# Multi-query attention on one core: the order of the queues comes from a virtual-time planner, and GpSimd's part of each cube is placed beside VectorE's passes over PSUM

## The chip, the core and the metric

The kernel runs on one core of a Trainium2 chip. A core has five engines that each work through a queue of their own: TensorE (PE in the profile; its weight loads are listed apart as PEld), VectorE (DVE), ScalarE (ACT), GpSimd (POOL) and SyncE (SP, which here only issues DMAs). They wait for each other through semaphores. SBUF is the on-chip memory that all engines and the DMAs use, PSUM the small accumulator memory that TensorE writes and VectorE and ScalarE read. The metric is the device time of one execution in microseconds; less is better. It is a little longer than the profile's span, which runs from the first to the last instruction of the program.

## The reference

Eight batches, 1024 positions, 16 query heads of 64, and one shared key and value head per batch:

```python
    q = q.transpose(0, 2, 1, 3)
    k = k[:, None, :, :].copy()
    v = v[:, None, :, :].copy()
    scores = np.matmul(q, k.transpose(0, 1, 3, 2)) / np.sqrt(head_dim)
    weights = np.exp(scores - np.max(scores, axis=-1, keepdims=True))
    weights = weights / np.sum(weights, axis=-1, keepdims=True)
    attn_out = np.matmul(weights, v)
    return attn_out.transpose(0, 2, 1, 3).astype(np.float32)
```

q is (8, 1024, 16, 64), k and v are (8, 1024, 64), all float32; the output has q's shape.

## The kernel before

**Steps.** The work is cut into 1024 steps u. A step is one pair of heads p (64 over all batches), one of two chunks c of 512 queries and one of eight tiles j of 128 keys. Eight steps of one pair and chunk make what is called a half here. In a step TensorE computes the scores of both heads (L261): two matmuls with 64 rows each into one PSUM tile `sc` of 128 keys x 2 heads x 512 queries. Such a tile takes two PSUM banks and there are three of them, so at most three steps' scores exist at a time. The scores leave TensorE transposed, keys on partitions, ready to be the weights of the second matmul. No maximum is subtracted; the sums of the weights are checked instead, and a slow general path stands ready behind a flag.

**Two ways to take the exponential.** ScalarE does it in one activation (L274) from `sc` to an fp16 tile `wt` (24 buffers). In every fifth step, 200 in all, VectorE does it with integer operations, which is called a unit here:

- bits (L215): scores plus an offset, from PSUM, written as int16; read as fp16 this is a rough power of two
- mantissa (L221) and power (L231): the mantissa and the exponent bits of that, by bit masks, from SBUF to SBUF
- square (L242): the mantissa times itself
- the cube: bits times square, 1024 columns of which GpSimd makes columns 512 to 1023 (L243) and VectorE columns 0 to 511 (L249, called rest below)

Bits, power and cube are three weight tiles in `w3` (6 buffers), and the values are kept three times, scaled by 1, C0 and C3 (L206, prep_v), so that three value matmuls add up to the exponential's. A step on ScalarE has one term, a unit three.

**Values.** A half has eight groups (4 blocks of 128 queries x 2 heads). Each sums its terms over the half's eight steps in matmuls of 128x65 (L335; the 65th column is the sum of the weights). Seven groups share a PSUM bank; two banks alternate. When seven are complete VectorE takes the reciprocals of the sums (L277, inverse) and multiplies (L286, finish) into `osb`, and SyncE stores what is complete, a half at a time. The last half is done apart (L365).

**Order.** Each engine's queue is in the order in which the program records its instructions. Before, this order is a fixed pattern: `step(u)` records the scores and the activation or the bits pass, then up to two pending VectorE operations; after three steps of every five (`DEAL`) a number of value matmuls worked out by `plan()` follows, some 18 scores behind (`LAG`). GpSimd's half of the cube is recorded with the square and starts whenever that is done.

**Next batch.** While a batch runs, the next one is loaded: keys and, on GpSimd's queue, values (L108) and eight q tiles (L125); SyncE transposes q by DMA (L135), and `prep_k` scales k on GpSimd into a doubled fp16 copy (L194, two instructions) which SyncE transposes (L198).

Of the kernel before, what the change touches and what calls it, by code (L numbers as in the profile page):

```python
# [24 lines left out]
DEAL = (1, 1, 0, 1, 0)  # L25
DEAL_AT = 1
VE_U = 512
VE_N = 1
VE_M = 5
# [3 lines left out]
def attention_main(ctx, tc, q, k, v, out, flag):  # L33
# [23 lines left out]
    OCH = 7  # L57
# [8 lines left out]
    wtp = ctx.enter_context(tc.tile_pool(name="wtp", bufs=24))  # L66
    w3p = ctx.enter_context(tc.tile_pool(name="w3p", bufs=6))
    mp = ctx.enter_context(tc.tile_pool(name="mp", bufs=2))
    osbp = ctx.enter_context(tc.tile_pool(name="osbp", bufs=2))
    chkp = ctx.enter_context(tc.tile_pool(name="chkp", bufs=2))  # L70
    scp = ctx.enter_context(tc.tile_pool(name="scp", bufs=3, space=PSUM))
# [9 lines left out]

    kv = {}
# [4 lines left out]
    ot = {}  # L87
    pend = []
    product = []
    late = []  # L90
    checked = [0]
# [98 lines left out]
    def prep_k(b):  # L190
        st = kv[b]
        k16d = kvp.tile([P, NKT, 2, D], FP16, tag="k16d", name=f"k16d_{b}")
        for i in range(2):
            nc.gpsimd.tensor_scalar(  # L194
                out=k16d[:, :, i, :], in0=st["knat"], scalar1=kscale, scalar2=None, op0=ALU.mult
            )
        st["k2t"] = kvp.tile([P, S], FP16, tag="k2t", name=f"k2t{b}")
        nc.sync.dma_start_transpose(  # L198
            out=st["k2t"].rearrange("p (j s) -> p j s", j=NKT),
            in_=k16d.rearrange("p j i d -> p (j i d)"),  # L200
        )

    def prep_v(b):
        vp = kv[b]["vp"]
        for i, ci in ((1, C0), (2, C3)):
            nc.vector.tensor_scalar(  # L206
                out=vp[:, i, :, 0:D], in0=vp[:, 0, :, 0:D], scalar1=ci, scalar2=None, op0=ALU.mult
            )

    def vector_exp(sc, p, c, j):  # L210
        w3 = w3p.tile([P, 3, 2, QCH], FP16, tag="w3", name=f"we{p}_{c}_{j}")
        m = mp.tile([P, 2, QCH], FP16, tag="m", name=f"m{p}_{c}_{j}")
        m2 = mp.tile([P, 2, QCH], FP16, tag="m2", name=f"mm{p}_{c}_{j}")
        t = w3[:, 1].bitcast(I16)
        nc.vector.tensor_scalar(  # L215
            out=t, in0=sc, scalar1=15.0 * 1024, scalar2=0.0, op0=ALU.add, op1=ALU.max
        )
        if product:
            pend.append(product.pop())
        pend.append(  # L220
            lambda: nc.vector.tensor_scalar(  # L221
                out=m.bitcast(I16),
                in0=t,
                scalar1=0x3FF,
                scalar2=0x3C00,
                op0=ALU.bitwise_and,
                op1=ALU.bitwise_or,
            )
        )
        pend.append(  # L230
            lambda: nc.vector.tensor_scalar(  # L231
                out=w3[:, 0].bitcast(I16),
                in0=t,
                scalar1=0x7C00,
                scalar2=None,
                op0=ALU.bitwise_and,
            )
        )
        we, wu, mm = (x.rearrange("p h q -> p (h q)") for x in (w3[:, 1], w3[:, 2], m2))

        def square():
            nc.vector.tensor_tensor(out=m2, in0=m, in1=m, op=ALU.mult)  # L242
            nc.gpsimd.tensor_tensor(  # L243
                out=wu[:, VE_U:], in0=we[:, VE_U:], in1=mm[:, VE_U:], op=ALU.mult
            )

        pend.append(square)
        product.append(
            lambda: nc.vector.tensor_tensor(  # L249
                out=wu[:, :VE_U], in0=we[:, :VE_U], in1=mm[:, :VE_U], op=ALU.mult  # L250
            )
        )
        wt[(p, c, j)] = [(w3[:, 0], 1), (w3[:, 1], 0), (w3[:, 2], 2)]

    def scores(p, c, j, by_vector):
        b = p // HP
        sc = scp.tile([P, 2, QCH], FP32, tag="sc", name=f"sc{p}_{c}_{j}")
        k2t = kv[b]["k2t"]
        for hh in range(2):
            r = 64 * hh  # L260
            nc.tensor.matmul(  # L261
                sc[:, hh, :],
# [6 lines left out]
        if by_vector:  # L269
            vector_exp(sc, p, c, j)  # L270
            return
        w = wtp.tile([P, 2, QCH], FP16, tag="wt", name=f"wt{p}_{c}_{j}")
        wt[(p, c, j)] = [(w, 0)]
        nc.scalar.activation(out=w, in_=sc, func=EXP, scale=escale, bias=math.log(CS))  # L274

    def inverse(o, g0, n):
        nc.vector.reciprocal(out=rec_all[:, g0 : g0 + n], in_=o[:, 0:n, D])  # L277

    def finish(o, g0, n):

        rec = rec_all[:, g0 : g0 + n]
        i0 = g0 % (OCH * GRP)
        if i0 == 0:
            osb[0] = osbp.tile([P, OCH * GRP, D], FP32, tag="osb", name=f"osb{g0}")
# [7 lines left out]
        while stored[0] < g0 + n:  # L292
            e = stored[0]
            e += GRP // 2 if e >= NG - GRP else GRP
# [4 lines left out]
        per = HP * NCH * GRP  # L299
        if g0 + n == NG:  # L300
            check(g0 - GRP // 2, NG, ok_all[:, B:])
        elif checked[0] < B and g0 + n >= min((checked[0] + 1) * per, NG - GRP):
            e = min((checked[0] + 1) * per, NG - GRP)
            b = checked[0]
            check(b * per, e, None, ok_all[:, b : b + 1])
            checked[0] += 1

    def store(ob, g0, g1):
# [3 lines left out]
        j0 = g0 % (OCH * GRP)  # L312
# [8 lines left out]
    def values(gg):  # L321


        p, c = divmod(gg // GRP, NCH)
        g = gg % GRP
        qb, hh = divmod(g, 2)
        if gg % GB == 0:
            ot[0] = bank(f"ot{gg}")[:, 0 : GB * 72].rearrange("p (g f) -> p g f", f=72)
        o = ot[0]
        vp = kv[p // HP]["vp"]  # L330
        terms = [(j, w, i) for j in range(NKT) for w, i in wt[(p, c, j)]]

        def one(n, j, w, i):
# [8 lines left out]
            if not last:  # L342
                return
# [316 lines left out]
```

## Time and profile before

| what | before |
|---|---|
| median of 3 runs | 775.24 us (774.51 to 775.27) |
| span of the profiled execution | 771.9 us |
| granted TensorE clock, mean | 0.995 |
| ScalarE: first and last exponential | 7.3 us, 765.9 us |
| GpSimd q loads, 64 | 38.4 us, 604 ns each |
| VectorE square / half-cube / mantissa / power, 200 each | 692 / 437 / 428 / 434 ns |
| VectorE finish, 145 of full size | 624 ns |
| GpSimd prep_k, 14 instructions | 23.0 us, 1652 ns each |

How to read it. A line of a group names the source line, engine, operation, out<-in tiles with shapes and the number of instructions; then the busy time, the mean duration of one in ns, and the idle time of the engine just before them with what ended most of it. The recorded durations of successive instructions of one engine overlap (by 164 ns on average for the exponentials, 1084 ns long and 920 ns apart), so an engine's cost is better taken from start to start in the timeline: a start, a duration, the engine, the instruction, and in brackets the idle time before it and who ended it. Matmuls overlap most: the recorded 190 ns of a value matmul is not its price. Over 100 to 700 us the stretches look alike:

```profile
100.00:300.00 200.00, 195.66 (x3587) 124.72 (x3583) 186.81 (x359) 199.40 (x218) 80.38 (x78) 1.00 0.53 98
300.00:500.00 200.00, 196.07 (x3596) 125.18 (x3595) 186.96 (x362) 199.64 (x219) 81.07 (x78) 1.00 0.56 98
500.00:700.00 200.00, 195.86 (x3584) 124.79 (x3580) 187.27 (x362) 199.46 (x219) 78.52 (x74) 1.00 0.49 91
```

The columns are the stretch, its length, the busy time (and instructions) of PE, PEld, DVE, ACT and POOL, then the granted clock, the share of the DMA engines and GB/s.

### The profile page before, as it was taken

Reading aid. Unit: us, or ns where it says so; the run is one execution under the profiler, and the core shown is the slowest. Engines: PE = TensorE matmul, PEld = TensorE weight load, DVE = VectorE, ACT = ScalarE, POOL = GpSimd, SP = SyncE. Lnnn points to the kernel's source line nnn. Section 1 sums busy time; section 2 is a strip of 40 time slices with the busy share of each in tenths; the row PEclk is TensorE's granted clock in tenths of the full one; section 3 lists DMA queues with packets and bytes.
Section 4 is the critical chain, followed back from the end, with each engine's and each line's share of the span. In section 5 each row is a group of like instructions: output and inputs, shape, how many; then the busy total and the mean of one; then the engine's idle time right before and its main releaser. Section 6 shows DMA issues by size and latency. Waiting matters only on the chain.

```text
span 771.9 us, 31242 instructions
## 1 busy us (share of the span) xinstructions
PE 741.9 (96%) x13474; PEld 471.0 (61%) x13474; DVE 695.4 (90%) x1349; ACT 759.3 (98%) x827; POOL 298.5 (39%) x299
## 2 busy tenths in 40 slices
PE   5999999999999999999999999999999999999997
PEld 1566666666666666666666666666666666666665
DVE  3899989998999998999899999999999999899993
ACT  7999999999999999999999999999999999999996
POOL 4453334533344333454234532345333443332330
PEclk9899999999999999999999999999999999999999
DMA  9858436764265533775356764467535665212113
GB/s 185 125 102 125 98 70 100 96 131 98 59 117 111 111 71 84 105 125 96 85 99 96 101 120 95 83 105 110 104 78 84 105 124 98 57 43 57 43 44 85
DMA packets 168637, 73.87 MB, mean 96 GB/s; under 512 B 93744, under 2 KB 161328, under 8 KB 168496
## 3 DMA queue, kind: packets, MB, share of 16 engines
q1 hardware_dynamic: 148864, 53.76, 34.1%
q0 software_dynamic: 18576, 17.57, 17.1%
q8 instruction: 106, 1.74, 1.0%
q10 hardware_dynamic: 1056, 0.52, 0.3%
q14 instruction: 35, 0.29, 0.1%
HBM read 37.75 MB, written 33.55 MB: 92 GB/s over the span
## 4 chain that ended last, share of the span: by engine, by line
PE 41%; ACT 34%; issue 13%; DVE 10%; DMA 1%; ACTq 0%; DVEq 0%
ACT wt L274 34%; PE ot L335 22%; PE sc L261 19%; DVE we L215 3%; DVE mm L242 2%; DVE osb L286 1%; DVE we L249 1%; DVE m L221 1%; DMA qf<-in_q_dram 1%; DVE ge L381 0%; DVE rec_all L277 0%; DMA out_dram<-osb 0%; PE otl L365 0%; DVE vp L206 0%; DVE both L387 0%
## 5 line engine op out<-in xcount | busy, mean ns | idle before, releaser
L274 ACT ACTIVATE wt<-sc 128x1024 f16<-128x1024 f32 x824 | 756.8, 1084 | 2.6 <-PE sc L261 2.4
L335 PE MATMUL ot<-vp,wt 128*128 128x65 f16 x6528 | 430.1, 194 | 0.8 <-DVE osb L286 0.7
L335 PEld LDWEIGHTS <-wt 128*128 128x128 f16 x6528 | 328.1, 98 | 134.7 <-issue 134.6
L243 POOL TENSOR_TENSOR we<-we,mm 128x512 f16<-128x512 f16 x200 | 230.8, 1154 | 442.8 <-DVE mm L242 208.6
L261 PE MATMUL sc<-qt,k2t 64*128 64x512 f16 x2048 | 362.7, 386 | 18.8 <-ACT wt L274 13.8
L335 PE MATMUL ot<-vp,we 128*128 128x65 f16 x4800 | 351.6, 193 | 0.0
L215 DVE TENSOR_SCALAR we<-sc 128x1024 int16<-128x1024 f32 x200 | 244.2, 1221 | 48.0 <-PE sc L261 45.3
L335 PEld LDWEIGHTS <-we 128*128 128x128 f16 x4800 | 251.6, 97 | 43.9 <-issue 43.8
L261 PEld LDWEIGHTS <-k2t 64*128 64x128 f16 x2048 | 85.7, 94 | 109.7 <-issue 76.6
L242 DVE TENSOR_TENSOR mm<-m 128x1024 f16<-128x1024 f16 x200 | 138.3, 692 | 0.1
L286 DVE TENSOR_TENSOR osb<-ot,rec_all 128x448 f32<-128x448 f32 x146 | 90.7, 622 | 5.1 <-DMA out_dram<-osb 0.2
L249 DVE TENSOR_TENSOR we<-we,mm 128x512 f16<-128x512 f16 x200 | 87.3, 437 | 0.0
L231 DVE TENSOR_SCALAR we<-we 128x1024 int16<-128x1024 int16 x200 | 86.7, 434 | 0.0
L221 DVE TENSOR_SCALAR m<-we 128x1024 int16<-128x1024 int16 x200 | 85.5, 428 | 0.0
L125 POOL DMA_DIRECT2D q<-in_q_dram x64 | 38.4, 604 | 10.6 <-DMA qt<-q 8.3
L277 DVE RECIPROCAL rec_all<-ot 128x7 f32<-128x7 f32 x146 | 28.5, 195 | 7.3 <-PE ot L335 7.2
L194 POOL TENSOR_SCALAR k16d<-knat 128x512 f16<-128x512 f32 x14 | 23.0, 1652 | 0.1
L108 POOL DMA_DIRECT2D vp<-in_v_dram x8 | 7.6, 952 | 0.0
L206 DVE TENSOR_SCALAR vp<-vp 128x512 f16<-128x512 f16 x16 | 4.8, 343 | 1.0 <-DMA vp<-in_v_dram 1.0
L159 PE MATMUL kps<-ident,k 128*64 128x128 f16 x16 | 1.3, 314 | 4.4 <-DVE k L150 4.4
L188 DVE COPY qt<-qps 128x512 f16<-128x512 f16 (+1 forms) x2 | 1.1, 556 | 3.8 <-PE qps L175 3.8
L381 DVE TENSOR_SCALAR ge<-rec_all 128x128 f32<-128x128 f32 (+2 forms) x9 | 3.8, 421 | 0.0
(30 smaller groups left out, 21.9 us busy)
## 6 DMA issues: line engine op xcount, KB each, us to landing
out_dram<-osb SPq DMA_DIRECT2D x127, 256.0 KB, 2.6
q<-in_q_dram POOLq DMA_DIRECT2D x56, 256.0 KB, 4.4
knat<-in_k_dram SPq DMA_DIRECT2D x7, 256.0 KB, 3.3
q<-in_q_dram POOLq DMA_DIRECT2D x8, 192.0 KB, 7.5
vp<-in_v_dram POOLq DMA_DIRECT2D x8, 128.0 KB, 4.7
qt<-q SPq DMA_TRANSPOSE x64, 4.6
qf<-in_q_dram ACTq DMA_DIRECT2D x2, 256.0 KB, 4.4
knat<-in_k_dram SPq DMA_DIRECT2D x2, 128.0 KB, 3.8
```

Source lines behind the costliest of these rows:

```text
L125: nc.gpsimd.dma_start(out=q16[(b, c)], in_=q[b, c * P : (c + 1) * P, h0:, :].rearrange("p h d -> p (h d)"),)
L215: nc.vector.tensor_scalar(out=t, in0=sc, scalar1=15.0 * 1024, scalar2=0.0, op0=ALU.add, op1=ALU.max)
L221: lambda: nc.vector.tensor_scalar(out=m.bitcast(I16), in0=t, scalar1=0x3FF, scalar2=0x3C00, op0=ALU.bitwise_and, op1=ALU.bitwise_or,)
L231: lambda: nc.vector.tensor_scalar(out=w3[:, 0].bitcast(I16), in0=t, scalar1=0x7C00, scalar2=None, op0=ALU.bitwise_and,)
L242: nc.vector.tensor_tensor(out=m2, in0=m, in1=m, op=ALU.mult)
L243: nc.gpsimd.tensor_tensor(out=wu[:, VE_U:], in0=we[:, VE_U:], in1=mm[:, VE_U:], op=ALU.mult)
L249: lambda: nc.vector.tensor_tensor(out=wu[:, :VE_U], in0=we[:, :VE_U], in1=mm[:, :VE_U], op=ALU.mult)
L261: nc.tensor.matmul(sc[:, hh, :], k2t[r : r + 64, j * P : (j + 1) * P], qt[b][r : r + 64, p % HP, c * QCH : (c + 1) * QCH], start=True, sto ...
L274: nc.scalar.activation(out=w, in_=sc, func=EXP, scale=escale, bias=math.log(CS))
L277: nc.vector.reciprocal(out=rec_all[:, g0 : g0 + n], in_=o[:, 0:n, D])
L286: nc.vector.tensor_tensor(out=ob[:, i0 : i0 + n, :], in0=o[:, 0:n, 0:D], in1=rec.unsqueeze(2).broadcast_to([P, n, D]), op=ALU.mult,)
L335: nc.tensor.matmul(o[:, gg % GB, 0 : D + 1], w[:, hh, qb * P : (qb + 1) * P], vp[:, i, j, 0 : D + 1], start=(n == 0), stop=last,)
```

## The change

The fixed pattern is replaced by `plan()`, which plays the whole kernel through in virtual time, with a price for every kind of instruction written at the top of the file, and records all instructions in the order of their virtual starts. Buffers are handed out by the planner too (rings `N_WT` 22 instead of 24, `N_W3` 7 instead of 6, squares 3, mantissas 2, three score tiles by number).

- **Which step goes to VectorE** is decided when its scores are issued (`issue`): at a rate of at most `RATE`, never two in a row, if VectorE's backlog is short enough. In the built order 223 units and 801 activations result. The last 12 steps are ScalarE's.
- **Scores** are issued when two slots are free, or when one is free and ScalarE would run out. The built order has 735 rounds of scores, 454 of one pair and most others of two, between 733 runs of values (605 and 602 before; 198 rounds of one pair).
- **Values** follow a new order of terms inside a group: first the one term (wt or bits) of all eight steps, then the power terms, then the cube terms. There are 11,696 value matmuls outside the last half (11,328 before).
- **The cube.** `share` gives GpSimd as many columns (a multiple of 32, at least 96) as fit between the end of one VectorE pass over SBUF and the start of the next, that is while VectorE reads PSUM (bits, inverse, finish). If that VectorE pass is not the unit's own square, the GpSimd instruction gets a dependency on it (`after_vector`), so that it doesn't start earlier. VectorE makes the columns that are left (`rest`). In the built order GpSimd has 229 shares with 144,320 columns (some 100 each of 864 and of 448 columns), VectorE 219 rests with 84,032 columns. Before it was 102,400 each.
- **VectorE's queue**: bits, inverse and finish are taken when they are due; mantissa, power, square, rest, prep and check fill in between. inverse is nearly always followed directly by finish (145 of 146).
- **The next batch**: `load_q` and `load_v` stay on GpSimd's queue and are recorded right behind a share; `prep_k` moves to VectorE as one instruction of 1024 columns; `check` is recorded apart.
- **Output** buffers hold 28 groups instead of 56, three instead of two; stores end at the buffer's end, so 36 more half-size stores appear.

The core of the diff:

```diff
-DEAL = (1, 1, 0, 1, 0)
-VE_U = 512
-VE_N = 1
-VE_M = 5
+N_WT = 22
+N_W3 = 7
+N_M = 2
+N_M2 = 3
+T_PAIR = 214.0
+T_IN = 96.0
+T_OUT = 106.0
+T_MM = 30.8
+T_SCORE = 480.0
+T_ACT = 917.0
...
+GP_START = 218.0
+GP_FIX = 58.0
+GP_COL = 1.887
+GP_TAIL = 230.0
+T_LOAD = {"load_q": 640.0, "load_v": 1000.0}
+SIDE = (("prep_k", 58), ("prep_v", 72))
+VE_COST = {
+    "bits": 1141.0,
+    "mantissa": 335.0,
+    "power": 335.0,
+    "square": 603.0,
...
+    "finish": 542.0,
+}
...
+RATE = 0.225
...
     def prep_k(b):
-        for i in range(2):
-            nc.gpsimd.tensor_scalar(
-                out=k16d[:, :, i, :], in0=st["knat"], scalar1=kscale, scalar2=None, op0=ALU.mult
-            )
+        x = nc.vector.tensor_scalar(
+            out=k16d,
+            in0=st["knat"].unsqueeze(2).broadcast_to([P, NKT, 2, D]),
...
+    def ve_cube(u, lo, hi, behind):
+        we, wu, mm = cube_of(u)
+        x = nc.gpsimd.tensor_tensor(
+            out=wu[:, lo:hi], in0=we[:, lo:hi], in1=mm[:, lo:hi], op=ALU.mult
+        )
+        if behind != ("square", u):
+            after_vector(x, behind)
+
+    def ve_rest(u, lo):
+        we, wu, mm = cube_of(u)
+        return nc.vector.tensor_tensor(
+            out=wu[:, lo:], in0=we[:, lo:], in1=mm[:, lo:], op=ALU.mult
+        )
+
+    def after_vector(x, key):
+        tc.add_manual_dep(
+            x.ins,
+            made[key].ins.name,
...
+    def terms_of(h):
+        us = range(h * NKT, (h + 1) * NKT)
+        own = [(u, 0) for u in us]
+        return own + [(u, i) for i in (1, 2) for u in us if kinds[u] == "V"]
...
+        def share(s):
...
+            v = next((v for v in left if left[v]), None)
+            if v is not None:
+                gs = max(t_gp, t_behind + GP_START, squared[v] + GP_START)
+                n = min(int((s - gs - GP_FIX) / GP_COL) // 32 * 32, left[v])
+                if n >= MINC:
+                    lo = 2 * QCH - left[v]
+                    emit(gs, "cube", v, lo, lo + n, behind)
+                    left[v] -= n
+                    lock = gs + GP_FIX + n * GP_COL
+                    t_gp = lock + GP_TAIL
...
+                    for x in loads:
+                        emit(t_gp, *x)
+                        t_gp += T_LOAD[x[0]]
+                    loads.clear()
...
+            to_v = (
+                first
+                and NKT <= u < STEPS - V_END
+                and not todo
+                and max(t_ve, s) + backlog() < s + T_SCORE + VE_SLACK
+                and kinds.get(u - 1) != "V"
+                and made_v < (u - NKT + 1) * RATE
+                and min(w3_used) < s
+            )
...
+            n_free = sum(f <= t_pe for f in free)
+            go = n_free > 1
+            if n_free == 1:
+                other = sorted(late_free(i) for i in range(3))[1]
+                go = max(other, t_pe) + T_IN + T_SCORE > t_act + WAIT and t_pe + NEAR >= t_act - T_IN - T_SCORE
...
+                if r <= t_pe:
+                    s = t_pe + (T_OUT if mode == "s" else 0)
+                    mode = "v"
+                    emit(s, "value", gg, n)
+                    t_pe = s + T_MM
...
+        return [(what, args) for _, _, what, args in sorted(ops, key=lambda x: x[:2])]
...
-        for u in range(STEPS):
-            step(u)
...
+        for what, args in plan():
+            x = run[what](*args)
+            if what in ("mantissa", "power", "square", "rest", "prep_k", "prep_v", "check"):
+                made[what, args[0]] = x
```

More of the change, by code (lines that the diff above doesn't have):

```diff
@@ L390, in check @@
         if all_ is not None:
[L391 to L393 removed]
+            return nc.vector.tensor_reduce(out=all_, in_=both, axis=AX.X, op=ALU.min)
     STEPS = NP * NCH * NKT
     PSTEPS = NCH * NKT
[L396 to L410 removed]
```

574 lines of the change are left out of this document (390 added, 184 removed).

## The prediction

> **What bounds the kernel now.** I read the page's busy shares first, then its costliest groups, then who waited for whom, then the timeline of one ordinary stretch, engine by engine.
>
> ```profile
> PE 741.9 (96%) x13474; PEld 471.0 (61%) x13474; DVE 695.4 (90%) x1349; ACT 759.3 (98%) x827; POOL 298.5 (39%) x299
> ...
> L274 ACT ACTIVATE wt<-sc 128x1024 f16<-128x1024 f32 x824 | 756.8, 1084 | 2.6 <-PE sc L261 2.4
> L335 PE MATMUL ot<-vp,wt 128*128 128x65 f16 x6528 | 430.1, 194 | 0.8 <-DVE osb L286 0.7
> L243 POOL TENSOR_TENSOR we<-we,mm 128x512 f16<-128x512 f16 x200 | 230.8, 1154 | 442.8 <-DVE mm L242 208.6
> L261 PE MATMUL sc<-qt,k2t 64*128 64x512 f16 x2048 | 362.7, 386 | 18.8 <-ACT wt L274 13.8
> L215 DVE TENSOR_SCALAR we<-sc 128x1024 int16<-128x1024 f32 x200 | 244.2, 1221 | 48.0 <-PE sc L261 45.3
> ```
>
> ScalarE's 824 exponentials cover 756.8 us and leave 2.6 us idle: it sets the pace. They overlap (1084 ns each, 1084 x 824 = 893 us), so their price is the step from start to start: 920 ns on average, 903 to 904 ns for two thirds of them. The bare floor is 7.3 us to the first + 824 x 0.9035 + 6.0 us after the last = 757.8 us; the span is 14 us above it. TensorE's 96% cannot be taken at its word, since its matmuls overlap too. Its real price is read from successive starts:
>
> ```profile
> 300.64 0.39 PE L261 MATMUL sc<-qt,k2t 64*128 64x512 f16 x2
> 300.96 0.39 PE L335 MATMUL ot<-vp,wt 128*128 128x65 f16 x7
> ...
> 301.57 0.60 PE L261 MATMUL sc<-qt,k2t 64*128 64x512 f16 x4
> 302.11 0.20 PE L335 MATMUL ot<-vp,wt 128*128 128x65 f16 x1
> ...
> 302.74 0.39 PE L261 MATMUL sc<-qt,k2t 64*128 64x512 f16 x2
> 303.35 0.39 PE L261 MATMUL sc<-qt,k2t 64*128 64x512 f16 x2 [0.21 <-ACT wt L274]
> ```
>
> The first line is a score pair, the next starts 16 values 0.32 us later, and 0.61 us after that the next pair starts. Two pairs follow: 0.54 us to the next value, so a second pair adds 0.22. The last two lines are also one round of two pairs, but 0.61 us apart: the second waited for ScalarE to free its PSUM slot. Over the whole trace, the means of steps without a wait are: value to value 31.6 ns, last value to pair 126, pair to value 309 (319 after two pairs), pair to pair 223, and 4 inside a pair. Before has 11,328 values in 602 runs and 1024 pairs in 605 rounds, so TensorE's need is 10,726 x 0.0316 + 602 x 0.126 + 602 x 0.316 + 419 x 0.223 + 1024 x 0.004 = 703 us. First to last score took 756 us. The difference, about 53 us, is TensorE waiting (some 9.5 us of it in the first 25 us), nearly all for ScalarE's slots. So time can be bought from ScalarE with TensorE's and VectorE's slack.
>
> ```profile
> 299.67 1.23 DVE L215 TENSOR_SCALAR we<-sc 128x1024 int16<-128x1024 f32 x1
> 300.81 0.48 DVE L249 TENSOR_TENSOR we<-we,mm 128x512 f16<-128x512 f16 x1
> 301.22 0.41 DVE L221 TENSOR_SCALAR m<-we 128x1024 int16<-128x1024 int16 x1
> 301.56 0.41 DVE L231 TENSOR_SCALAR we<-we 128x1024 int16<-128x1024 int16 x1
> 301.89 0.68 DVE L242 TENSOR_TENSOR mm<-m 128x1024 f16<-128x1024 f16 x1
> 302.50 0.19 DVE L277 RECIPROCAL rec_all<-ot 128x7 f32<-128x7 f32 x1
> 302.72 0.62 DVE L286 TENSOR_TENSOR osb<-ot,rec_all 128x448 f32<-128x448 f32 x1
> 303.26 1.21 DVE L215 TENSOR_SCALAR we<-sc 128x1024 int16<-128x1024 f32 x1
> ```
>
> The steps here are VectorE's prices: the pass over scores 1.14 us, mantissa and power 0.335 each (medians; here 0.34 and 0.33), square 0.602 (median), reciprocal 0.22, finish 0.54. The half-cube usually takes 0.332; here it took 0.41.
>
> **The change part by part.**
>
> *23 units move from ScalarE to VectorE* (counted in the built order: 801 activations, 223 vector units). ScalarE's need falls by 23 x 0.920 = 21.2 us. If nothing else ended last, the span would be 771.9 - 21.2 = 750.7 us.
>
> *TensorE gets more to do.* Each unit adds two terms to each of 8 groups: 23 x 16 = 368 values, 11.6 us. The planner also cuts the scores into smaller rounds: the built order has 735 score rounds (455 or so of one pair, the others mostly of two) and 733 value runs. Need: (11,696 - 733) x 0.0316 = 346.4; 733 x 0.126 = 92.4; 454 x 0.309 + 279 x 0.319 = 229.3; (1024 - 735) x 0.223 = 64.4; inside pairs 4.1. Sum 736.6 us, 34 us more than before. Around it stand 6.6 us to the first score, the start, where only ScalarE paces (first value after 9 scores instead of 18; I take 6 us, between 4 and the 9.5 of before), and 8.3 us from the last values to the end (763.6 to 771.9 in the trace: last 64 values, eviction, check, closing branch). TensorE alone: 6.6 + 736.6 + 6 + 8.3 = 757.5 us. That is above ScalarE's 750.7: TensorE becomes the bound. This also fits the order: the first value of a step's weights now stands some 14 to 21 scores behind its score, against 11 to 18 before, so values lag as far as the weight rings allow and seldom wait for fresh data.
>
> *VectorE.* 223 x (1.14 + 2 x 0.335 + 0.602) = 537.9. The rest of the cube is now 84,032 columns in 219 instructions; square and half-cube, the same operation at 1024 and 512 columns, give 0.062 us + 0.527 ns per column, so 57.9. 146 evictions x 0.76 = 111; 8 checks 6.6; prep_v 3. prep_k comes from GpSimd, 7 x 1024 columns from fp32; its nearest row on VectorE is the first k scaling at 0.294 us per 256 columns, which gives at most 1.2 us each, and the 16-bit 1024-column mantissa pass at least 0.335; I take 0.7, 5 us in all. Sum 721 us, against 669 before. Its stretch runs from 13 us (ninth score) to about 20 us before the end (last unit is score 1011 of 1023), with some 4 us of evictions behind it: 13 + 721 - 4 + 20 = 750 us. It fits with 8 us to spare.
>
> *GpSimd.* Its fixed 512-column half becomes 229 shares, mostly of 864 or 448 columns, 144,320 columns in all, each told to start only after a named VectorE instruction. Priced by column from its row (1152 ns per 512) this is 325 us; if the price were all fixed, 229 x 1.15 = 263. Both are far under the span; what counts is when a share runs. The 0.48 us half-cube above shows why: a cube that started at 299.87 was still running, and VectorE lost 0.08. The trace has 50 such stretched passes, 11 us in all, of which about 7 us come from prep_k's 14 GpSimd instructions (mantissa, power and square stretched by 0.4 us at a time). Those leave GpSimd, so this loss should fall to some 4 us even if the new placing did nothing. The Trainium skill's page "SBUF — State Buffer", section "Who interferes with whom", gives the mechanism: VectorE's fast one-input passes, and its two-input ones against GpSimd reads, share a port pair with GpSimd as an exclusive lock, and whoever starts first blocks the other for its whole instruction. The trace agrees in kind (power 820 ns beside prep_k, 419 alone).
>
> *Queues.* The 64 q loads and 7 v loads are now issued on GpSimd right behind a share; 0.6 and 0.95 us each in their rows, as before. Waiting behind them is the next share, and behind that the third weight term, which TensorE uses 13 or more scores (over 9 us) later: hidden. The Trainium skill's page "SBUF — State Buffer", section "SBUF: two separate sides", warns against this place: such a DMA can take about 3.1 us instead of 0.62 when VectorE's two-port passes keep GpSimd from writing descriptors; by it, as an estimate, 71 loads would hold GpSimd 176 us longer and push shares into rival 3. The trace differs: the loads that ran beside mantissa and power passes took 0.53 to 0.80 us. Stores split more often (28-group buffers, three of them); the DMA engines are about half idle, so I price that at nothing; without that cover finish would wait for a buffer, as it did once for 0.2 us.
>
> *Sum.* Largest of 757.5 (TensorE), 750.7 (ScalarE), 750 (VectorE), plus waits of TensorE for slots that none of these contain. Before lost 14 us above its floor with two slack engines; here all three lie within 8 us, but the bounding engine runs late against the plan and so finds slots free. I take 2.5 us, with 0 and 14 as bounds: span 760. The median of runs is 775.24 - 771.9 = 3.3 us above the profiled span: 763 us.
>
> **The rivals.**
> 1. *TensorE is not in the way.* If my step prices contain hidden waits (the 31.6 ns could be 29, its commonest value: 10,963 x 2.6 ns = 28 us), ScalarE stays the bound: 750.7 + 3.3 = 754 us. Against it: value steps average 30 to 31 at every place in a run, with no waits shown on them. Chance 0.1.
> 2. *No gain: three saturated engines on three PSUM slots.* A late vector pass holds a slot, ScalarE runs dry, and the delay is passed round. If the waits equal before's 14 us, 757.5 + 14 + 3.3 = 775 us. For it: 45.3 us of VectorE's waits for scores are already there. Against: values lag more, rings are deep. Chance 0.08; part falls within no change.
> 3. *Slower: shares collide.* A share of 864 columns lasts up to 1.94 us by column. If its VectorE partner is not over PSUM then (score late, load ahead of the share), VectorE's next pass over SBUF can be stretched by up to the whole of it (prep_k's 1.65 us instructions stretched one by 0.4 and the next by 0.4); I take 1 us. VectorE has 8 us of slack, then each collision lengthens the span: the gain is gone at 8 + 14 = 22 collisions, one share in ten; with one in five (46) the time is 750 + 46 + 3.3 = 799, and one in seven gives 786. For it: an order fixed ahead, without reacting to lateness, and shares sized to fill the pass. Against: shares start on VectorE's own signal, and only 25 of 200 cubes stretch a pass now, by 0.11 us. Chance 0.12.
> 4. *The change doesn't do what it says*: the order holds 801 and 223, so this is left at nothing.
>
> **How the numbers follow.** My forecast, TensorE the bound with few waits, has 0.70: 757 to 771 us. Two in ten outside: range 756 to 779. The measurement tells about 0.2% (1.6 us) from no change, so faster means under 773.7: 0.70 + 0.10 and a little of rival 2 = 0.81; within 0.2% 0.05; slower 0.14.
>
> **What would show it.** Right: ScalarE at 801 activations with clearly more idle time than 2.6 us, ended by scores; TensorE's pair to pair waits down from about 50 us to under 15; VectorE over 94% busy; mantissa, power and square near 419, 419 and 683 ns. Wrong: square or power means far above these (rival 3); TensorE waiting long for VectorE's slots (rival 2) or values waiting for the third term; value steps under 30 ns (rival 1).

## The result and the profile after

The changed kernel takes 769.33 us (median of 4 runs, 769.12 to 769.76) against 775.24 before: 0.9927 of the time, with a 95% interval of 0.9913 to 0.9941. That is 5.9 us faster. The forecast was 763 us, 12.2 us faster; the range of 756 to 779 holds the result. The profiled execution has a span of 767.5 us, 4.4 us less than before's 771.9. Wherever an execution has both numbers on record, it takes 1.7 to 2.0 us more than its span; so 771.9 would belong to an execution of some 773.8 us, faster than before's median.

First the page's busy shares, then its chain of the work that ended last, then its costliest groups:

```profile
PE 753.1 (98%) x13842; PEld 486.4 (63%) x13842; DVE 733.0 (96%) x1467; ACT 748.6 (98%) x804; POOL 360.0 (47%) x314
...
PE 95%; ACT 2%; DVE 1%; DMA 1%; issue 0%
...
L276 ACT ACTIVATE wt<-sc 128x1024 f16<-128x1024 f32 x801 | 746.1, 1040 | 4.5 <-PE sc L263 3.6
L319 POOL TENSOR_TENSOR we<-we,mm 128x864 f16<-128x864 f16 (+5 forms) x229 | 315.4, 1377 | 386.3 <-DVE mm L315 148.2
L396 PE MATMUL ot<-vp,wt 128*128 128x65 f16 x6344 | 441.3, 194 | 0.0
L396 PE MATMUL ot<-vp,we 128*128 128x65 f16 x5352 | 431.3, 194 | 0.0
...
L263 PE MATMUL sc<-qt,k2t 64*128 64x512 f16 x2048 | 353.0, 386 | 3.5 <-ACT wt L276 2.8
L283 DVE TENSOR_SCALAR we<-sc 128x1024 int16<-128x1024 f32 x223 | 272.0, 1220 | 6.0 <-PE sc L263 4.3
...
L294 DVE TENSOR_SCALAR m<-we 128x1024 int16<-128x1024 int16 x223 | 95.1, 427 | 0.3
L304 DVE TENSOR_SCALAR we<-we 128x1024 int16<-128x1024 int16 x223 | 93.4, 419 | 0.0
```

The busy shares alone say that three engines are full. The chain says which of them decides. Before, the same line of the page read

```profile
PE 41%; ACT 34%; issue 13%; DVE 10%; DMA 1%; ACTq 0%; DVEq 0%
```

because the end was reached by way of TensorE waiting for ScalarE's slots; now 95% of it is TensorE's own work. Score matmuls idle 3.5 us where they idled 18.8, value matmuls 0.0. VectorE's idle time ahead of its bits passes fell from 48.0 to 6.0 us; the part that scores ended fell from 45.3 to 4.3. The windows over the middle of the run, with the columns of the section on before, show the same in 200 us stretches:

```profile
100.00:300.00 200.00, 200.00 (x3715) 129.57 (x3712) 196.67 (x394) 199.37 (x214) 97.87 (x83) 1.00 0.55 98
300.00:500.00 200.00, 200.00 (x3714) 129.67 (x3711) 197.20 (x394) 198.69 (x214) 94.77 (x80) 1.00 0.58 100
500.00:700.00 200.00, 200.00 (x3712) 129.44 (x3708) 197.34 (x395) 199.04 (x215) 95.16 (x78) 1.00 0.53 91
```

TensorE is never idle and does 3.5% more matmuls per stretch than before (about 3714 against 3590). ScalarE looks as busy as before (199 of 200), but with 214 or 215 activations where there were 218 or 219: its steps now last 936 ns on average instead of 920, which is waiting that overlapping records hide.

TensorE's ordinary round, from its timeline, has one pair and 17 values; the start of each line is what counts:

```profile
301.66 0.39 PE L263 MATMUL sc<-qt,k2t 64*128 64x512 f16 x2
301.98 0.33 PE L396 MATMUL ot<-vp,we 128*128 128x65 f16 x5
...
302.62 0.39 PE L263 MATMUL sc<-qt,k2t 64*128 64x512 f16 x2
```

The pair costs 0.32 us up to the first value, and 0.64 us later the next pair starts. This is the same pattern as before, without the waits. Counted over the whole trace from start to start, the terms of the prediction came out as follows (us):

| term | predicted | after's trace |
|---|---|---|
| 10,963 steps from value to value | 346.4 (31.6 ns each) | 351.4 (32.05 ns) |
| 733 steps from the last value to a pair (732 in the trace) | 92.4 | 93.5 |
| 733 steps from the last pair to a value | 229.3 | 231.5 |
| pair to pair, inside pairs, ScalarE-paced start | 74.5 | 75.8 |
| up to the first score | 6.6 | 6.7 |
| from the last value to the end | 8.3 | 8.7 |
| allowance for waits | 2.5 | inside the rows above |
| sum, to be the span | 760.0 | 767.6 |

### The profile page after: what moved, and what is told of

Same layout as the page of the kernel before. It is cut to its first block, busy times and chain, and to the rows that moved or that the text cites. A ratio compares the mean times of both kernels' runs of the same rounds, so it can differ in the third digit from the quotient of the medians.

```text
span 767.5 us, 31677 instructions
## 1 busy us (share of the span) xinstructions
PE 753.1 (98%) x13842; PEld 486.4 (63%) x13842; DVE 733.0 (96%) x1467; ACT 748.6 (98%) x804; POOL 360.0 (47%) x314
## 4 chain that ended last, share of the span: by engine, by line
PE 95%; ACT 2%; DVE 1%; DMA 1%; issue 0%
PE ot L396 57%; PE sc L263 38%; ACT wt L276 2%; DMA qf<-in_q_dram 1%; DVE we L283 0%; PE otl L420 0%; DVE osb L354 0%; PE qps L216 0%; DVE rec_all L345 0%; ACT q_first L799 0%; DVE mm L315 0%; ACT qt L229 0%; DVE we L304 0%; DVE m L294 0%; PE cnt L837 0%
## 5 line engine op out<-in xcount | busy, mean ns | idle before, releaser
L276 ACT ACTIVATE wt<-sc 128x1024 f16<-128x1024 f32 x801 | 746.1, 1040 | 4.5 <-PE sc L263 3.6
L319 POOL TENSOR_TENSOR we<-we,mm 128x864 f16<-128x864 f16 (+5 forms) x229 | 315.4, 1377 | 386.3 <-DVE mm L315 148.2
L396 PE MATMUL ot<-vp,wt 128*128 128x65 f16 x6344 | 441.3, 194 | 0.0
L396 PE MATMUL ot<-vp,we 128*128 128x65 f16 x5352 | 431.3, 194 | 0.0
L396 PEld LDWEIGHTS <-we 128*128 128x128 f16 x5352 | 313.0, 97 | 92.0 <-issue 89.7
L263 PE MATMUL sc<-qt,k2t 64*128 64x512 f16 x2048 | 353.0, 386 | 3.5 <-ACT wt L276 2.8
L283 DVE TENSOR_SCALAR we<-sc 128x1024 int16<-128x1024 f32 x223 | 272.0, 1220 | 6.0 <-PE sc L263 4.3
L315 DVE TENSOR_TENSOR mm<-m 128x1024 f16<-128x1024 f16 x223 | 152.4, 683 | 0.1
L294 DVE TENSOR_SCALAR m<-we 128x1024 int16<-128x1024 int16 x223 | 95.1, 427 | 0.3
L304 DVE TENSOR_SCALAR we<-we 128x1024 int16<-128x1024 int16 x223 | 93.4, 419 | 0.0
L327 DVE TENSOR_TENSOR we<-we,mm 128x160 f16<-128x160 f16 (+5 forms) x219 | 78.2, 357 | 0.1
L166 POOL DMA_DIRECT2D q<-in_q_dram x64 | 38.6, 604 | 2.1 <-DMA q_first<-in_q_dram 1.7
```

The costliest lines, as they stand in the source:

```text
L166: nc.gpsimd.dma_start(out=q16[(b, c)], in_=q[b, c * P : (c + 1) * P, h0:, :].rearrange("p h d -> p (h d)"),)
L263: nc.tensor.matmul(sc[u][:, hh, :], k2t[r : r + 64, j * P : (j + 1) * P], qt[b][r : r + 64, p % HP, c * QCH : (c + 1) * QCH], start=True, ...
L276: nc.scalar.activation(out=w, in_=sc.pop(u), func=EXP, scale=escale, bias=math.log(CS))
L283: nc.vector.tensor_scalar(out=w3[:, 1].bitcast(I16), in0=sc.pop(u), scalar1=15.0 * 1024, scalar2=0.0, op0=ALU.add, op1=ALU.max,)
L294: return nc.vector.tensor_scalar(out=ve[u]["m"].bitcast(I16), in0=ve[u]["w3"][:, 1].bitcast(I16), scalar1=0x3FF, scalar2=0x3C00, op0=ALU.b ...
L304: return nc.vector.tensor_scalar(out=ve[u]["w3"][:, 0].bitcast(I16), in0=ve[u]["w3"][:, 1].bitcast(I16), scalar1=0x7C00, scalar2=None, op0 ...
```

## The experiments

Three questions were open: is it TensorE that sets the time; why did its steps get dearer; and what is the placing of GpSimd's shares worth. The times below are medians, the ratios are to the kernel before on the same chip, with 95% intervals. Before took 774.1 to 774.4 us beside the experiments and 775.2 beside the change, so a time of an experiment against the change's 769.33 is uncertain by about 1 us.

| kernel | median us | ratio | span us |
|---|---|---|---|
| the change | 769.33 | 0.9927 [0.9913, 0.9941] | 767.5 |
| e1: TensorE does less | 757.24 | 0.9776 [0.976, 0.9793] | 755.4 |
| e2: VectorE without squares | 781.3 | 1.0092 [1.0075, 1.0109] | 778.9 |
| e3: value rows 72 apart | 761.27 | 0.9827 [0.981, 0.9843] | 759.3 |
| e4: old order of terms | 763.86 | 0.9861 [0.9845, 0.9878] | 762.3 |
| e5: shares not tied to VectorE | 847.1 | 1.094 [1.0921, 1.0958] | 847.4 |
| e6: 206 units | 769.72 | 0.9946 [0.993, 0.9963] | 767.2 |
| e7: before, value rows 72 apart | 773.58 | 0.9991 [0.9982, 1.0001] | 772.3 |
| e8: value rows 96 apart | 759.52 | 0.981 [0.9793, 0.9826] | 757.6 |
| e9: e8, planner's prices new, 221 units | 758.91 | 0.9806 [0.9789, 0.9822] | 757.6 |
| e10: e9 with 211 units | 764.43 | 0.9883 [0.9866, 0.9899] | 762.5 |
| e11: value rows 68 apart | 762.83 | 0.985 [0.9834, 0.9866] | 761.4 |
| e12: e8, old order of terms | 759.39 | 0.9803 [0.9787, 0.982] | 758.3 |

### Is TensorE the bound? (e1, e7, e2)

**e1** takes work from TensorE alone (what it computes is then no longer the attention; its time is all that is used):

```diff
     def value(gg, n):
...
+        if i == 0 and u % NKT == 3:
+            return
```

> The changed kernel without the value matmuls of key tile 3's first term (1016 of 11,696 values; ScalarE, VectorE and GpSimd do all that they did). Theory T (TensorE alone bounds the changed kernel): 1016 x 32 ns = 32.5 us less to do, so the time falls from 769.3 until the next engine ends last; by ScalarE's steps (7.3 + 801 x 0.904 to 0.920 + 6 = 737 to 750) and VectorE's sum (750) that is a time of 745 to 758 us. Rival V (VectorE, 96% busy, bounds) and rival S (ScalarE's steps themselves became longer, 936 ns against 920): no change, 767 to 771 us.

Measured: 757.24 us. Removing 1016 value matmuls, about 32 us of TensorE's steps, saves 12 us and then something else is in the way. That something is read from e1's chain of the page and from its window of the middle:

```profile
DVE 47%; ACT 26%; PE 16%; issue 6%; DMA 3%; POOL 0%; SPq 0%; DVEq 0%; ACTq 0%
```

```profile
300.00:500.00 200.00, 197.96 (x3501) 127.50 (x3499) 198.39 (x401) 199.54 (x218) 94.85 (x80) 1.00 0.59 102
```

TensorE falls to 16% of the chain; VectorE and ScalarE, both near 200 of 200 us, take its place. So in the changed kernel TensorE decides, and the next floor lies some 12 us below it.

**e7** makes TensorE's value steps cheaper in the kernel before, where ScalarE was said to be the bound (how is told with e3):

```diff
-    vps = [consts.tile([P, 3, NKT, 66], FP16, name=f"vp{i}") for i in range(2)]
+    vps = [consts.tile([P, 3, NKT, 72], FP16, name=f"vp{i}") for i in range(2)]
```

> The kernel before the change, with rows of the values tile 72 elements apart instead of 66, nothing else. Its TensorE has some 50 us of waits, so 5 to 9 us less TensorE work should not show if ScalarE is its bound (theory T): 773 to 776 us, less than 0.3% from before. If TensorE's step price was already part of before's bound (rival U): 766 to 771 us, as much gained as in the changed kernel.

Measured: 773.58 us, ratio 0.9991, an interval that holds 1. Its value steps took 334.9 us in all instead of 338.9, and the time did not follow. Before was not bound by TensorE; after is.

**e2** was to take load from VectorE, by leaving out the squares (the cube then uses the mantissa, which gets six buffers; the result is not the attention's):

```diff
     def ve_square(u, i):
...
-        m = ve[u].pop("m")
-        return nc.vector.tensor_tensor(out=ve[u]["m2"], in0=m, in1=m, op=ALU.mult)
+        ve[u]["m2"] = ve[u].pop("m")
+        return made["mantissa", u]
```

> The changed kernel without VectorE's 223 squares (602 ns each, 134 us of VectorE's time; the cube uses the mantissa instead, in six buffers instead of two plus three). TensorE, ScalarE and GpSimd do as much as before. Theory T: VectorE is not the bound, the time stays at 768 to 770 us. Rival V: at least 10 us less, under 760 us. Rival S: no change either.

Measured: 781.3 us, slower than both kernels, which neither theory had. A miss in the design: without the square, shares that waited for it start right behind the mantissa pass and run into the power pass. Two lines of e2's groups show it (the same lines of after read 3.5 us idle, and 93.4 us, 419 ns each):

```profile
L263 PE MATMUL sc<-qt,k2t 64*128 64x512 f16 x2048 | 353.7, 386 | 12.4 <-DVE we L283 7.9
...
L304 DVE TENSOR_SCALAR we<-we 128x1024 int16<-128x1024 int16 x223 | 149.6, 671 | 0.0
```

VectorE was busy only 89% of that span, so the run says nothing on whether VectorE is a bound. What it shows is the harm of late passes: VectorE had 41 us less work in all (691.6 us against 733.0), and yet the kernel took longer, with TensorE now waiting for VectorE's slots. What such collisions cost without the missing square, e5 measures.

### Why did the value steps get dearer? (e4, e3, e8, e11, e12)

A value matmul's step (start to start) is 29 or 30 ns in four of ten cases in the changed kernel and 32 to 36 ns in most others; before, it was 29 or 30 ns in over half. Which it is depends on which row of the values comes after which, as a count over the traces shows. In the changed kernel the step after row 1, 2, 3, 5, 6 or 7 of the unscaled copy is never under 31 ns (33.5 on average, 5724 steps), while after rows 0 and 4 and after scaled rows it is mostly 29 or 30 (30.3 and 30.5 on average). In before's trace the same six rows cost 33.6 ns into any row but a cube's, and 29.7 ns into a cube's (1175 steps). Before, a unit's three terms stood together, so that many unscaled rows were followed by a cube row. The new order puts the unscaled terms of all eight steps behind each other, and no unscaled row is followed by a cube row any more. **e4** goes back to the old order and lets the planner plan again:

```diff
     def terms_of(h):
         us = range(h * NKT, (h + 1) * NKT)
-        own = [(u, 0) for u in us]
-        return own + [(u, i) for i in (1, 2) for u in us if kinds[u] == "V"]
+        return [(u, i) for u in us for i in ((1, 0, 2) if kinds[u] == "V" else (0,))]
```

> The changed kernel with the terms inside a group in the old order (tile by tile: power, bits, cube together) instead of all first terms, then powers, then cubes; the planner plans anew with it. Theory T with the step price set by which term follows which: the mean step goes from 32.05 back to 31.6 ns or a little less, TensorE needs 5 us less, 762 to 767 us. If the order of terms has no part in it: 768 to 771 us, with 32.05 ns. If cube terms are now needed too early, TensorE waits for GpSimd and the time rises above 771 us.

Measured: 763.86 us, with a mean step of 31.57 ns, which is before's price. Value steps sum to 346.2 us, the prediction's 346.4. In e4's trace 1390 steps lead from one of the six rows to a cube row, at 30.1 ns on average instead of 33.5; this alone is 1390 x 3.4 ns = 4.7 of the 5.2 us between the two sums. That the time is the prediction's 763 as well is partly luck: e4's span of 762.3 is 2.3 us above the 760 forecast, and the 3.3 us added there are 1.8. **e3** changes instead how far apart the value rows lie in SBUF, 72 fp16 elements instead of 66:

```diff
-    vps = [consts.tile([P, 3, NKT, 66], FP16, name=f"vp{i}") for i in range(2)]
+    vps = [consts.tile([P, 3, NKT, 72], FP16, name=f"vp{i}") for i in range(2)]
```

> The changed kernel with rows of the values tile 72 elements apart instead of 66, nothing else. In the trace a step from value to value takes 29 ns when the first of the two reads row 0 or 4 of the unscaled values, or any row of the scaled ones, and mostly 32 to 35 ns for rows 1, 2, 3, 5, 6, 7; rows 0 and 4 are those that begin on a multiple of 16 bytes. Theory R (the row's start sets the step): with all rows on multiples of 16 bytes all steps are 29 to 30 ns, TensorE needs 10,963 x 2 = 20 us or more less and the time falls to 746 to 756 us. Rival W (the step is set by which weights follow which, rows have no part): steps stay at 32.05 ns on average, the time at 768 to 771 us.

Measured: 761.27 us, between the two theories. The differences between rows are gone: the step is now 29 or 30 ns in seven of ten cases and 35 or 36 ns in about one of five, whatever the rows. After scaled rows it even became slower (31.1 ns on average instead of 30.5). So the distance matters, but not simply as "aligned is fast". **e8** (96 elements apart) and **e11** (68) try two more distances, and **e12** is e8 with e4's order:

> The changed kernel with rows 96 elements apart (192 bytes, a multiple of 64). With 72 (144 bytes) the mean step was 31.27 ns instead of 32.05, with one step in five at 35 ns whatever the row. Theory R2 (the rest of the long steps also comes from where a row starts, within 32 or 64 bytes): most of the 35s go, the mean falls to 30.5 ns or less and the time to 750 to 757 us. Rival R3 (multiples of 16 bytes are all that matters, the 35s come from something else): as with 72, 760 to 763 us.

> The changed kernel with rows 68 elements apart (136 bytes; only every second row begins on a multiple of 16 bytes, every row on one of 8). If starting on a multiple of 16 bytes is what counts: between 66 and 72 elements, mean step about 31.6 ns, 764 to 766 us. If any distance other than 66 ends the long steps: as with 72, 759 to 762 us. If half of the rows are as slow as rows 1 to 3 are now: no gain, 768 to 771 us.

> The changed kernel with rows 96 elements apart and the old order of terms together. Theory A (the order of terms costs 5 us only because with rows 66 apart the step's price depends on which row follows which): with 96 the order makes no difference, mean step 31.1 ns, 758 to 761 us. Rival B (the order has a price of its own, such as fewer changes between weight buffers): another 5 us off, 753 to 756 us, mean step under 30.8 ns.

Measured: 759.52, 762.83 and 759.39 us. e8 lies just below the range for the case that the 35 ns steps stay, and they do stay. Its trace shows that they go by the place in a run of values: the first two steps after scores are always slow, then the 3rd to 5th never, the 7th in 90% of the runs, the 8th to 10th almost never, the 12th in 92%. e11's time falls between two of its stated outcomes, but its steps decide between them. With 68, rows 2 and 6 begin on a multiple of 16 bytes too (counted from the start of the tile), and the step after them, unscaled, falls from 33.2 to 29.8 ns; after rows 1, 3, 5 and 7 it is never under 32 ns, 33.8 on average, as with 66. So for the unscaled copy the start of the row decides. The scaled rows begin at the same distances from such a multiple and yet stay at 30.5 ns in both kernels; why is open. (The edit also moves what lies behind this tile in SBUF; that just the rows named change speaks against that as the cause.) e12 is as e8: at 96 elements the order of terms is worth nothing, so it matters only through the distance of the rows. What joins these runs is a subtraction:

| kernel | mean value step, ns | sum of value steps, us | span, us | span minus sum |
|---|---|---|---|---|
| the change (66) | 32.05 | 351.4 | 767.5 | 416.1 |
| e4 (66, old order) | 31.57 | 346.2 | 762.3 | 416.1 |
| e11 (68) | 31.51 | 345.4 | 761.4 | 416.0 |
| e3 (72) | 31.27 | 342.8 | 759.3 | 416.5 |
| e12 (96, old order) | 31.20 | 342.0 | 758.3 | 416.3 |
| e8 (96) | 31.11 | 341.1 | 757.6 | 416.5 |

The last column is the same within 0.5 us while the sums differ by 10 us. Every microsecond of value steps is a microsecond of the kernel, which is what "TensorE is the bound" means. The window over the middle shows the same from the other side: TensorE is as full in e8 as in the change, and does 3767 matmuls in 200 us instead of 3714.

```profile
300.00:500.00 200.00, 199.92 (x3767) 128.98 (x3763) 198.09 (x400) 199.06 (x217) 94.68 (x79) 1.00 0.59 102
```

### What is the placing of GpSimd's shares worth? (e5)

**e5** leaves sizes and recorded order as they are and takes away only the added dependency on a VectorE pass:

```diff
         x = nc.gpsimd.tensor_tensor(
             out=wu[:, lo:hi], in0=we[:, lo:hi], in1=mm[:, lo:hi], op=ALU.mult
         )
-        if behind != ("square", u):
-            after_vector(x, behind)
```

> The changed kernel without the added dependencies: GpSimd's shares start as soon as their data is there, as before the change, and no longer behind a named VectorE pass; sizes and order are the same. Theory P (the placing is what lets VectorE carry 223 units): shares run into VectorE's passes over SBUF, mantissa, power and square are stretched by up to a share's length (1 to 2 us for 864 columns) as in the run without the square, VectorE loses more than the 10 to 20 us it has to spare and the time rises to 775 us or more. Rival Q (the placing has little part; before the change only 25 of 200 half-cubes stretched a pass, by 0.11 us): 768 to 772 us.

Measured: 847.1 us, 78 us slower than the change and 73 us slower than before. First the busy shares, the chain and the power line on e5's page, then four lines of its timeline:

```profile
PE 766.0 (90%) x13842; PEld 499.2 (59%) x13842; DVE 814.5 (96%) x1467; ACT 761.7 (90%) x804; POOL 367.0 (43%) x314
...
DVE 74%; PE 11%; issue 10%; DMA 3%; ACT 2%; DVEq 0%; SPq 0%
...
L304 DVE TENSOR_SCALAR we<-we 128x1024 int16<-128x1024 int16 x223 | 162.3, 728 | 0.0
```

```profile
301.46 0.41 DVE L294 TENSOR_SCALAR m<-we 128x1024 int16<-128x1024 int16 x1
301.62 1.15 POOL L319 TENSOR_TENSOR we<-we,mm 128x448 f16<-128x448 f16 x1 [1.45 <-DVE mm L315]
301.79 1.25 DVE L304 TENSOR_SCALAR we<-we 128x1024 int16<-128x1024 int16 x1
302.97 1.21 DVE L283 TENSOR_SCALAR we<-sc 128x1024 int16<-128x1024 f32 x1
```

With the same instructions VectorE is busy 81.5 us longer than in the change (814.5 against 733.0), and 69 of these are power passes: 55 of the 223 last over 0.5 us, 1.25 us longer on average than the usual 0.42. In the timeline the share starts at 301.62 as soon as its square is done and ends at 302.77. The power pass, which starts at 301.79, ends 0.27 us after that: it takes 1.25 us instead of 0.42. In the changed kernel's timeline a share waits until VectorE is over PSUM:

```profile
302.87 0.42 DVE L304 TENSOR_SCALAR we<-we 128x1024 int16<-128x1024 int16 x1
303.27 1.23 DVE L283 TENSOR_SCALAR we<-sc 128x1024 int16<-128x1024 f32 x1
...
304.41 0.20 DVE L345 RECIPROCAL rec_all<-ot 128x7 f32<-128x7 f32 x1
304.64 0.62 DVE L354 TENSOR_TENSOR osb<-ot,rec_all 128x448 f32<-128x448 f32 x1
305.18 0.23 DVE L327 TENSOR_TENSOR we<-we,mm 128x160 f16<-128x160 f16 x1
```

```profile
303.46 1.82 POOL L319 TENSOR_TENSOR we<-we,mm 128x864 f16<-128x864 f16 x1 [1.82 <-DVE we L304]
```

It runs from 303.46 to 305.28, beside bits, inverse and finish, which all read PSUM and all keep their usual durations; VectorE makes the remaining 160 columns as it ends. GpSimd idled 1.82 us for that, and this costs nothing. The Trainium skill's page "SBUF — State Buffer", section "Who interferes with whom", describes such a lock, held for a whole instruction by whoever starts first; e5's power pass, which finishes only after the share has, agrees with it.

### How many units? (e6, e9, e10)

**e6** lowers the planner's `RATE` from 0.225 to 0.205: 206 units, 818 activations, 272 value matmuls fewer and 701 score rounds.

> The changed kernel with a rate of 0.205 instead of 0.225: 206 units, 818 activations, 11,424 values in 701 score rounds (735 before this edit). By TensorE's steps its need falls by 272 x 0.032 + 32 x 0.27 = 17 us or a little less (16 of 743 by the count); ScalarE gets 17 activations more, 15 us. Theory T (TensorE alone bounds; the last 17 units cost it more than ScalarE gains): ScalarE's steps go back toward 920 ns, 7.3 + 818 x 0.904 to 0.920 + 6 gives 753 to 766 us of span, a time of 755 to 766 us, below 769. Rival S (ScalarE sets the pace at 936 ns for reasons of its own): 818 x 0.936 + 13 + 2 = 781 us.

Measured: 769.72 us, as the change, and outside both expectations. Its chain of the page and two lines of its waits (us in total, times, longest) say why:

```profile
ACT 61%; PE 31%; issue 6%; DVE 1%; DMA 1%; ACTq 0%
```

```profile
DVE we L283 <- PE sc L263: 50.3, 84, 1.5
...
PE sc L263 <- ACT wt L276: 8.6, 26, 0.5
```

ScalarE paces the kernel again, as before the change: 7.4 us to its first exponential + 818 x 0.920 + 6.8 us after its last = 767 us, its span. The 0.920 is the mean step with its waits; at the 0.904 of a step without waits the sum would be 754, so some 13 us are waits, where before the change had 14. VectorE's waits for scores are back at 50 us. So 206 and 223 units stand on the two sides of the balance, and that they give the same time is a coincidence of two different limits. **e9** has rows 96 apart, prices in the planner taken from these traces, and a rate of 0.22; **e10** is the same at 0.21.

```diff
-T_PAIR = 214.0
-T_IN = 96.0
-T_OUT = 106.0
-T_MM = 30.8
+T_PAIR = 222.0
+T_IN = 92.0
+T_OUT = 100.0
+T_MM = 31.1
...
-T_ACT = 917.0
+T_ACT = 904.0
...
-RATE = 0.225
+RATE = 0.22
...
-WAIT = 50.0
+WAIT = 120.0
```

> The changed kernel with rows 96 elements apart and the planner's prices set to what the traces show (ScalarE's step 904 ns instead of 917, value 31.1 instead of 30.8, second pair 222, ways in and out of a round 92 and 100), waiting a little longer for a second slot (120 ns instead of 50), rate 0.22: 221 units, 715 score rounds. TensorE's need by its steps falls by another 5 us against the run with rows 96 apart (733 to 728). Theory T (TensorE still bounds, without waits): 759.5 - 5, 753 to 756 us. Rival B (once TensorE's need comes near ScalarE's 803 x 0.904 + 13 = 739 and VectorE's 750 us, the three pass waits round, as with 206 units, where 17 us were lost): 757 to 762 us, with waits of TensorE for slots of 5 us or more.

> The same with rate 0.21: 211 units, 813 activations, 706 score rounds. TensorE's need falls by 6 us more, ScalarE's floor rises by 9 to 748 us. Theory T alone gives 748 to 751 us; with ScalarE's floor and some waits 753 to 758 us; rival B 760 us or more.

Measured: 758.91 us with 221 units and 764.43 with 211, so the hoped-for 753 to 756 was not reached; both lie where their rival B put them. In e9 some 20 score rounds fewer save about 4 us of TensorE's steps (20 x (0.126 + 0.32 - 0.223 - 0.032)), but its waits at the step from values into a pair grew from 2 us in e8 to about 6. e9 beats the kernel before by 15 us and the change by 10, but its interval overlaps that of e8 and e12: the new prices and the rate, which were changed together, bring nothing beyond the row distance that can be told from noise.

## Why the forecast was right in kind and too large in size

**What bound the kernel before: right.** Cheaper value steps leave before's time alone (e7) and lower that of after one for one (the table of differences).

**TensorE becomes the bound: right, and with fewer waits than allowed for.** Between 100 and 700 us it waited 0.05 us ahead of pairs, against 36 us before (steps longer than the usual ones); over the whole trace its only wait for a cube was

```profile
PEld L396 <- POOL we L319: 2.1, 6, 0.4
```

Of the prediction's signs, ScalarE's idle time rose only from 2.6 to 4.5 us, since its overlapping records hide most of its waits; its longer steps (936 ns) show them.

**The step that failed is "(11,696 - 733) x 0.0316 = 346.4".** It measured 351.4, 5.0 us more, the largest single part of the 7.5 us by which the span exceeded the 760 forecast. The price was before's mean over all value steps. But the change reorders the terms in a group, which the prediction described and used only for how far values lag; it did not price the step by which row follows which, though before's trace had both prices in it (33.6 and 29.7 ns after the same rows). Where the order alone is put back (e4), the value steps are 346.2 us. Nor do they average 30 to 31 ns "at every place in a run": in before's trace the first step after scores averages 38.8 ns and the second 35.1.

**The other terms** add 5.1 us to the forecast: 2.2 for pair to value, where two prices had been exchanged (319 ns after one pair, 309 after two), 1.1 for last value to pair, 1.3 for the rest of the pairs and the start, 0.5 for both ends. Against that stands the 2.5 us allowed for waits, since any waits are already in those terms. Together 5.0 + 5.1 - 2.5 = 7.6 us (the two spans differ by 7.5); and the median lies 1.8 us above the span, not 3.3, which set before's median beside the span of a faster execution: 763 + 7.5 - 1.5 = 769. That mistake happened to hide 1.5 us of the miss.

**Where ScalarE's 21 us went.** Before had 53 us of slack on TensorE. The change spends some 41 us of it: 368 values more are 11.6 us, 130 score rounds more 130 x (0.126 + 0.316 - 0.223 - 0.032) = 24.3 (a further round adds a step into the scores and one out of them, and takes away one from pair to pair and one from value to value), dearer value steps 5.0. Of the other 12 us, 8 to 9 are still waits, most of them in the first 25 us, and the rest is the 4 us by which the span fell. So of ScalarE's 21 us little arrives. The two needs from 206 to 223 units show the same exchange: ScalarE saves 17 x 0.920 = 15.6 us, and TensorE pays 272 x 0.0316 + 34 x 0.187 = 15.0.

**VectorE's 750 us: near the truth.** It is busy 197 of 200 us and, once TensorE has room (e1), it ends last, with ScalarE.

**The placing of the shares: its cost was right, its worth was missed.** "So this loss should fall to some 4 us even if the new placing did nothing" is refuted by e5: with the placing gone the loss is 78 us, where the 50 stretched passes of before cost 11 us. Larger shares and a fuller VectorE are the likely reason, which no run separates. Rival 3's mechanism is therefore real and its price of 1 us a collision too low (1.25 in e5, on 55 of 223 power passes); in the changed kernel it did not occur because the dependency starts each share on VectorE's own signal, the argument given against it. In after VectorE's mantissa and power passes last 427 and 419 ns, close to the 419 expected.

**Rival 1** (steps of 29 ns, 754 us) went the other way, since the steps became longer. **Rival 2** (three engines on three slots) is not seen in the changed kernel. With fewer units it is: e6 and e10 lie 13 us above ScalarE's need at 0.904 us a step (754 and 750 us), VectorE waits 50.3 and 35.8 us for scores and TensorE 8.6 and 7.2 us for ScalarE's slots. Which of these waits starts the round, no run shows.

## What to carry to other kernels

Price a step by the pair of instructions that will stand behind each other in the new order, not by the mean of the old one; on an engine that is about to become the bound, 0.5 ns times 11,000 is 5 us, nearly as much as the whole gain that was measured. When one engine's work is bought with another's, work out both ends of the exchange: here 206 and 223 units give the same 769 us, and a one-line change of the row distance then gives 10 us more because it touches the engine that decides. A GpSimd instruction that can hold up VectorE's passes over SBUF is worth delaying by a dependency until VectorE is over PSUM.

## What the runs showed of the hardware that was not expected

- The time of a value matmul (65 columns fp16) depends on where its moving rows lie and on which row came before: 29 to 35 ns, on average 32.05 ns with rows 66 elements apart, 31.51 with 68, 31.27 with 72 and 31.11 with 96. With rows 66 and 68 apart, the step after an unscaled row that does not begin on a multiple of 16 bytes is 33 to 34 ns on average, unless a cube row follows (29.7 to 30.1); the scaled rows do not show this, and why is open. Where all rows begin on such a multiple (72 and 96), about every fifth step of a run still takes 35 ns, whatever the rows.
- A GpSimd share that started ahead of VectorE's power pass held that pass up until the share had ended (1.25 us instead of 0.42). With 55 of 223 power passes held up, e5 takes 78 us more than the change.
- GpSimd's DMA issues right behind a share cost no more than before: 64 q loads take 38.6 us, 604 ns each. The 3.1 us that the prediction quoted from the Trainium skill's page "SBUF — State Buffer", section "SBUF: two separate sides", do not show in this.
